# Bonus products and the group norm's transposes, issued after whole projections, in a one-core hybrid decoder layer

## The chip, the cores and the metric

The kernel runs on one core of one Trainium2 chip. The metric is the device time of one execution in microseconds (us). Its engines are named as the profile names them: PE (TensorE, matmuls and transposes), PEld (its weight loads), DVE (VectorE), ACT (ScalarE), POOL (GpSimd), and SP, which here only issues DMAs.

## The reference

One decoder layer over 512 tokens of width 1024, all in float32:

```
h      = rms_norm(x) * (1 + scale) + shift            # scale, shift from c
proj   = h @ w_in                                     # r, k, v, three low-rank inputs, conv u1/u2, gates a/b
r,k,v  = token_shift(proj[...])
y_a    = group_norm(rwkv7_scan(r, decay, k, v, -kk, kk*a)) * gn_gain + gn_bias
bonus  = sum_per_head(r * k * r_k) * v
y_a    = (y_a + bonus) * g
y_b    = silu(layer_norm(causal_conv31(u1 * sigmoid(u2))))
x      = x + gate * (concat(y_a, y_b) * sigmoid(gates)) @ w_out
x      = x + gate * relu(rms_norm(x)... @ w_ff_in)^2 @ w_ff_out
out    = rms_norm(x)
```

The change is about two lines of this: the bonus (a sum over each head of 64 channels, times v) and the group norm's output.

## The kernel before

The activations lie with channels on the 128 partitions and the 512 tokens along the free dimension. A **projection** (`proj`, L458) makes 128 output channels: two weight loads from HBM of 256 KB each into `raw_*`, a split of each into a high and a low part (`hi_*` on ACT, `lo_*` on POOL or DVE, L150 and L151), and then `mm3` (L163): 24 matmuls of 128x512 into one PSUM tile `ps_*` (lines 174, 175, 176 in turn, 8 times).

The 16 heads are worked on as 8 **pairs** j of two heads (128 channels), and two pairs make a **quarter** q of four heads. `rkv_pair(j)` makes the decay input `pzz` (L493), then the projections k, v, r of the pair, each followed by the token shift (`shift`, L464: ACT L465, then DVE L466). `prep_pair(j)` then forms, through small matmuls `pl` (L509), `pa` (L517) and `pn` (L524) and a chain of ACT and DVE instructions (L513 to L537), the scan's operands `AR` and `BK`, and last the **bonus**: L537 multiplies r, r_k and k into the tile `tr`; L539 is the matmul `pb`, which sums over each head with the block matrix `blk1` (`blk` in the trace); L541 multiplies by v into `bo`; L542 sends `bo` to the DRAM tile `bod[j]`. `tr` and `bo` have one buffer each (`bo` shares its tag `w1` with a tile that the next pair writes at L522).

For a quarter, `products` (L547) multiplies `AR` and `BK` into PSUM tiles `pA` (two banks, four chunks each, twice per pair) and masks them on DVE into `M` (L567); `solve` (L580) inverts small triangular blocks on DVE (62 instructions at L598 and L600); `merge_inverses`, `scan_operands` and `scan` follow, and `group_norm` (L707): statistics on DVE, 16 ACT instructions at L719 that normalise the tile `yq`, and then for each of the two pairs four transposes `pyt` (L724), a load of `bod[j]` (L726), one DVE instruction (L727) and a store to the DRAM tile `yad[j]` (L729), which `gate_a(j)` loads later.

The PSUM tag `m` of pool `pq` has two buffers. Of the loop's tiles, `pzz`, `pl`, `pa`, `pn`, `pb` and `pA` take them; `pyt` shares the one buffer of tag `y` with the scan's output `py`.

The order of the steps is a hand-written list, `ORDER` (L35): R is `rkv_pair`, I `products`, V `solve`, O `scan_operands`, M `merge_inverses`, S `scan`, Y `group_norm`, U two convolution projections (`u2`, then `u1`), T the 30 convolution taps on DVE (`cz`, L745), G `gate_a` with one projection `ga`, N, B, L, A, W later steps. It begins

```
U1:0v R0 R1:0v I0 U4 R2:0v R3 V0 T1:500 U3 M0 O0 T4 S0:2000 U2:0v I1:100 V1 O1:200 M1 T3:2000 Y0 R4
R5 G0 T2 U6:100 I2 V2:200 G1 S1:500 T6 U7 Y1 R6 M2 O2 R7 T7 I3:1000 V3:1000 U5 S2:100 O3 Y2 U0:100
```

The program is traced in this order; a number after a colon moves a step's instructions ahead by so many places. A planner then writes, before the program runs, one fixed list of instructions for each engine and for SP's DMA queue: it takes the earliest-traced instruction whose inputs it holds to be ready, by costs of its own. On the chip each engine runs its list in that order and waits where an input is late.

The functions that the change touches, and what calls them:

Of the kernel before, what the change touches and what calls it, by code (L numbers as in the profile page):

```python
# [8 lines left out]
F32 = mybir.dt.float32  # L9
# [3 lines left out]
ALU = mybir.AluOpType  # L13
# [5 lines left out]
P = 128  # L19
T = 512  # L20
# [42 lines left out]
def tile_rwkv7_conformer(  # L63
# [5 lines left out]
    nc = tc.nc  # L69
    V, S, G, PE = nc.vector, nc.scalar, nc.gpsimd, nc.tensor  # L70
# [14 lines left out]
    blk1 = const.tile([P, P], F32, name="blk1")  # L85
# [36 lines left out]
    hh = hp.tile([P, KT, T], F32R, name="hh")  # L122
    hl = hp.tile([P, KT, T], F32R, name="hl")
# [6 lines left out]
    def rsqrt_small(dst, v, tmp):  # L130

        V.tensor_scalar(dst.bitcast(I32), v.bitcast(I32), -0.5, 1597463007.0, op0=ALU.mult, op1=ALU.add)
        for _ in range(3):
            V.tensor_tensor(tmp, dst, dst, op=ALU.mult)
            V.scalar_tensor_tensor(tmp, tmp, -0.5, v, op0=ALU.mult, op1=ALU.mult)
            V.scalar_tensor_tensor(dst, tmp, 1.5, dst, op0=ALU.add, op1=ALU.mult)
# [17 lines left out]
    def wcol(src, c0, nm, eng=None, own=None):  # L154
        v = src.rearrange("(g k p) n -> g p k n", p=P, k=HK)
        out_ = []
        for g in range(2):
            raw = wp.tile([P, HK, P], F32, tag="wraw", name=f"raw_{nm}{g}")
            nc.sync.dma_start(out=raw, in_=v[g, :, :, c0:c0 + P])
            out_.append(split(raw, [P, HK, P], f"{nm}{g}", eng, own))  # L160
        return out_

    def mm3(ps, w, m):  # L163

        for k in range(KT):
            last = mm3k(ps, w, m, k)
        return last

    def mm3k(ps, w, m, k, ts_=slice(0, T), first=None):
        mh, ml = m  # L170
        wh, wl = w[k // HK]
        i = k % HK
        first = k == 0 if first is None else first
        PE.matmul(ps[:, ts_], wh[:, i, :], mh[:, k, ts_], start=first, stop=False, skip_group_check=True)  # L174
        PE.matmul(ps[:, ts_], wh[:, i, :], ml[:, k, ts_], start=False, stop=False, skip_group_check=True)  # L175
        return PE.matmul(ps[:, ts_], wl[:, i, :], mh[:, k, ts_], start=False, stop=(k == KT - 1),  # L176
                         skip_group_check=True)
# [9 lines left out]
    bod = [dram.tile([P, T], F32, name=f"bod{j}") for j in range(KT)]  # L187
# [55 lines left out]
    pq = cq.enter_context(tc.tile_pool(name="pq", bufs=1, space=PSUM, reuse_waits="tile"))  # L243
# [3 lines left out]
    with tc.tile_pool(name="e1", bufs=1) as e1, tc.tile_pool(name="e2", bufs=2) as e2:  # L247
# [11 lines left out]
        def load_ada(j):  # L259
            for s, o in ((1, D), (0, 0)):  # L260
# [19 lines left out]
                        op=ALU.add, axis=AX.X)  # L280
# [35 lines left out]
        for n, _, tag in EARLY:  # L316
            early[n] = (pq if tag == "y" else pp).tile([P, T], F32, tag=tag, name=f"ps_{n}",
                                                       bufs=2 if tag == "pp" else 1)
# [107 lines left out]
        for op in EORD.split():  # L426
            op, hp = (op + ":0").split(":")[:2]
# [25 lines left out]
    with ExitStack() as c1:  # L453
        lp = c1.enter_context(tc.tile_pool(name="lp", bufs=1, reuse_waits="tile"))
        qp = cq.enter_context(tc.tile_pool(name="qp", bufs=1, reuse_waits="tile"))
        tp = tpool[0] = cq.enter_context(tc.tile_pool(name="tp", bufs=1, reuse_waits="tile"))

        def proj(c0, nm):  # L458
            w = wcol(w_in2, c0, nm, lo_eng[0])
            ps = pp.tile([P, T], F32, tag="pp", name=f"ps_{nm}", bufs=2)  # L460
            mm3(ps, w, (hh, hl))
            return ps

        def shift(dst, ps, m):  # L464
# [15 lines left out]
        def chunks(t_):  # L480
            return t_.rearrange("p (c s) -> p c s", s=C)
# [22 lines left out]
        def prep_pair(j, rt, kt, vv, sg, WA):  # L504
            jc = slice(j, j + 1)

            pl = pq.tile([P, T], F32, tag="m", name=f"pl{j}", bufs=2)
            for tt in range(NT):
                PE.matmul(pl[:, tt * P:(tt + 1) * P], sg[:, tt, :], tri, start=True, stop=True)  # L509
            Pt = tp.tile([P, NCHK, 65], F32, tag="Pt", name=f"Pt{j}")  # L510
            Pi = tp.tile([P, NCHK, C], F32, tag="Pi", name=f"Pi{j}")
            G.memset(Pt[:, :, 0:1], 1.0)  # L512
            S.activation(Pt[:, :, 1:65], chunks(pl), AF.Exp, scale=-0.5 * ECON)  # L513
            S.activation(Pi, chunks(pl), AF.Exp, scale=0.5 * ECON)

            pa = pq.tile([P, T], F32, tag="m", name=f"pa{j}", bufs=2)
            PE.matmul(pa, WA[64:128, :], lo2[64:128, :], start=True, stop=True)  # L517
            at = tp.tile([P, T], F32, tag="sg", name=f"at{j}")
            S.activation(at, pa, AF.Tanh, bias=a0h[:, jc], scale=0.5)

            w1 = tp.tile([P, T], F32, tag="w1", name=f"w1_{j}")
            S.activation(w1, kt, AF.Square, scale=VEC["k_k"][:, jc])  # L522
            pn = pq.tile([P, T], F32, tag="m", name=f"pn{j}", bufs=2)
            PE.matmul(pn, blk1, w1, start=True, stop=True)  # L524
            S.activation(w1, pn, AF.Ln)
            S.activation(w1, w1, AF.Exp, scale=-0.5)
            V.scalar_tensor_tensor(w1, w1, 1e12, kt, op0=ALU.min, op1=ALU.mult)
            AR = qp.tile([P, NCHK, P], F32, tag="AR", name=f"AR{j}", bufs=4)
            BK = qp.tile([P, NCHK, P], F32, tag="BK", name=f"BK{j}", bufs=BKB)
            V.scalar_tensor_tensor(AR[:, :, 0:C], chunks(w1), kkn[:, jc], Pt[:, :, 0:C], op0=ALU.mult, op1=ALU.mult)  # L530
            V.scalar_tensor_tensor(w1, at, 1.0, w1, op0=ALU.add, op1=ALU.mult)
            V.scalar_tensor_tensor(BK[:, :, 0:C], chunks(w1), kkh[:, jc], Pi, op0=ALU.mult, op1=ALU.mult)
            S.activation(at, at, AF.Identity, scale=kah[:, jc], bias=ka1[:, jc])
            V.tensor_tensor(kt, kt, at, op=ALU.mult)
            V.tensor_tensor(BK[:, :, C:P], chunks(kt), Pi, op=ALU.mult)
            V.tensor_tensor(AR[:, :, C:P], chunks(rt), Pt[:, :, 1:65], op=ALU.mult)
            V.scalar_tensor_tensor(rt, rt, VEC["r_k"][:, jc], kt, op0=ALU.mult, op1=ALU.mult)  # L537
            pb = pq.tile([P, T], F32, tag="m", name=f"pb{j}", bufs=2)
            PE.matmul(pb, blk1, rt, start=True, stop=True)  # L539
            bo = tp.tile([P, T], F32, tag="w1", name=f"bo{j}")  # L540
            V.tensor_tensor(bo, pb, vv, op=ALU.mult)  # L541
            nc.sync.dma_start(out=bod[j], in_=bo)  # L542
            pc = qp.tile([P, NCHK, 1], F32, tag="pc", name=f"pc{j}", bufs=4)
            G.tensor_copy(pc, Pt[:, :, 64:65])
            return dict(AR=AR, BK=BK, v=vv, pc=pc, j=j)
# [161 lines left out]
        def group_norm(q, prs, yq, st):  # L707
            mv = qp.tile([P, NT * 4, 2], F32, tag="mv", name=f"mv{q}")
            rsd = qp.tile([P, NT * 4, 1], F32, tag="rsd", name=f"rsd{q}")
            for tt in range(NT):  # L710
                for h in range(4):
                    V.bn_aggr(mv[:, 4 * tt + h, :], st[:, tt, h:h + 1, :])
            rst = qp.tile([P, NT * 4, 1], F32, tag="rst", name=f"rst{q}")
            V.tensor_scalar(mv[:, :, 1:2], mv[:, :, 1:2], 64e-5, None, op0=ALU.add)
            rsqrt_small(rsd, mv[:, :, 1:2], rst)
            yv = yq.rearrange("p a h n -> p (a h) n")
            V.scalar_tensor_tensor(rst, mv[:, :, 0:1], -1.0, rsd, op0=ALU.mult, op1=ALU.mult)
            for i in range(NT * 4):
                S.activation(yv[:, i, :], yv[:, i, :], AF.Identity, scale=rsd[:, i, :], bias=rst[:, i, :])  # L719
            for pr, d in enumerate(prs):  # L720
                j = d["j"]
                pt = pq.tile([P, NT, P], F32, tag="y", name=f"pyt{q}{pr}")
                for tt in range(NT):
                    PE.transpose(pt[:, tt, :], yq[:, tt, 2 * pr:2 * pr + 2, :].rearrange("p h n -> p (h n)"), ident)  # L724
                yg = tp.tile([P, T], F32, tag="gy", name=f"yg{j}")
                nc.sync.dma_start(out=yg, in_=bod[j])  # L726
                V.scalar_tensor_tensor(yg, pt.rearrange("p a b -> p (a b)"), VEC["gn_gain"][:, j:j + 1], yg,  # L727
                                       op0=ALU.mult, op1=ALU.add)
                nc.sync.dma_start(out=yad[j], in_=yg)  # L729
# [259 lines left out]
        for op in ORDER.split():  # L989
            op, hp = (op + ":0").split(":")[:2]  # L990
# [5 lines left out]
    with tc.tile_pool(name="s3", bufs=2, reuse_waits="tile") as s3:  # L996
# [45 lines left out]
        for fq in range(NFQ):  # L1042
            fh = s3.tile([P, KT, T], F32R, tag="fh", name=f"fh{fq}")
            fl = s3.tile([P, KT, T], F32R, tag="fl", name=f"fl{fq}")
            for i in range(KT):
                if fq == 0 and i < NFF:
                    ps = first_ff[i]
                else:
                    w = wcol(w_ff_in[0], fq * D + i * P, f"fi{fq}{i}", G if fq == 0 and GFI > i else None)
                    ps = pp.tile([P, T], F32, tag="pp", name=f"ps_fi{fq}{i}", bufs=2)  # L1050
                    mm_last = mm3(ps, w, (hh, hl))
                f = s3.tile([P, T], F32, tag="f", name=f"f{fq}{i}")
# [8 lines left out]
            last = fq == NFQ - 1  # L1061
# [48 lines left out]
```

## Time and profile before

| what | value |
|---|---|
| median of 3 runs | 1126.58 us (1123.9 to 1131.93) |
| the profiled execution: its own time, and its span from the first to the last instruction | 1131.94 us, 1130.2 us |
| mean granted TensorE clock | 0.953 of full |
| PE busy, and PEld | 1023.5 us (91%), 792.5 us (70%) |
| DVE busy | 790.1 us (70%) |
| ACT, POOL busy | 479.1 us (42%), 198.2 us (18%) |
| DMA, mean over the span | 116 GB/s |

A row of the timeline has a start (us from the span's start), a duration (us), the engine, the line, the operation, the tile written and the tiles read, shapes and a count; in square brackets stands how long the engine was idle before it and what ended that. Neighbouring instructions of one line are merged into one row. A row of waits has the waiting instruction, what it waited for, the time in total, how many times and the longest. The four parts of the span are the load and first norm (up to about 75 us), the mixing layer's projections and scans (to about 600), the output projection with loads of the adaLN weights (to about 775), and the MLP.

### The profile page before, as it was taken

The page shows a single profiled execution, that of the slowest core. Times are in us where ns is not written, and L with a number is a line of the kernel's source. Part 1 is how long each engine was busy: PE and PEld are TensorE (multiplying, and loading weights), DVE is VectorE, ACT ScalarE, POOL GpSimd, SP SyncE. Part 2 cuts the span into 40 slices and gives each one's busy share as a digit, 9 for nine tenths or more (in the row PEclk, how much of TensorE's full clock was granted, in tenths as well). Part 3 has the DMA queues.
Part 4 walks back from the last instruction along what each step waited for, and adds up shares of the span by engine and source line. Part 5 has one row for each costly group of instructions (what it writes and reads, how often), then busy time and mean ns, then how long its engine had stood idle before and what let it go on. Part 6 is the DMA issues. An engine that isn't in the chain of part 4 may idle for free.

```text
span 1130.2 us, 16757 instructions
## 1 busy us (share of the span) xinstructions
PE 1023.5 (91%) x6037; PEld 792.5 (70%) x6037; DVE 790.1 (70%) x1622; ACT 479.1 (42%) x912; POOL 198.2 (18%) x191
## 2 busy tenths in 40 slices
PE   2999889889899789996997999899999999999995
PEld 1777666656677666665665767688888888888874
DVE  3859999969958997989455787585445445445557
ACT  5546445374644356534343433264323323423432
POOL 1123042222422533221121121200000000000002
PEclk9999999989999989996798999999999999999998
DMA  9622332331343234324257686731223323333332
GB/s 313 181 72 87 88 100 73 54 92 48 104 117 94 86 95 83 85 66 110 94 162 234 224 273 217 232 104 38 84 93 95 101 94 94 95 93 100 96 103 74
DMA packets 184605, 131.34 MB, mean 116 GB/s; under 512 B 49945, under 2 KB 152779, under 8 KB 184523
## 3 DMA queue, kind: packets, MB, share of 16 engines
q1 hardware_dynamic: 184523, 130.28, 39.1%
q8 instruction: 47, 0.77, 0.3%
q14 instruction: 35, 0.29, 0.1%
HBM read 116.61 MB, written 13.63 MB: 115 GB/s over the span
## 4 chain that ended last, share of the span: by engine, by line
PE 43%; DVE 16%; DMA 5%; issue 3%; ACT 3%; POOL 1%; SPq 0%; DVEq 0%; ACTq 0%; POOLq 0%
PE ps_fi L174 5%; PE ps_fi L175 5%; PE ps_fi L176 5%; DVE cz L745 5%; PE acc_fo L1005 4%; PE acc_fo L1004 4%; PE acc_fo L1003 4%; DMA ar<-in_ada_w_dram 2%; DVE tmp L598 1%; DVE aacc L217 1%; PE ps_ga L175 1%; PE ps_ga L176 1%; PE ps_ga L174 1%; DVE X L600 1%; PE pr L669 1%
## 5 line engine op out<-in xcount | busy, mean ns | idle before, releaser
L745 DVE SCALAR_TENSOR_TENSOR cz<-gl,cw,cz 128x512 f32<-128x512 f32 x240 | 200.8, 837 | 3.9 <-ACT cz L743 1.2
L151 DVE TENSOR_TENSOR lo_fo<-raw_fo,hi_fo 128x512 fp32r<-128x512 f32 x64 | 44.2, 691 | 92.1 <-ACT hi_fo L150 91.9
L175 PE MATMUL ps_fi<-hl,hi_fi 128*128 128x512 f32 (+1 forms) x288 | 105.6, 367 | 0.0
L176 PE MATMUL ps_fi<-hh,lo_fi 128*128 128x512 f32 (+1 forms) x288 | 105.3, 367 | 0.0
L174 PE MATMUL ps_fi<-hh,hi_fi 128*128 128x512 f32 (+1 forms) x288 | 105.0, 367 | 0.0
L1003 PE MATMUL acc_fo<-hi_fo,fh 128*128 128x512 f32 x256 | 101.3, 396 | 0.8 <-DVE t_fo L1010 0.8
L1004 PE MATMUL acc_fo<-lo_fo,fh 128*128 128x512 f32 x256 | 101.2, 395 | 0.0
L1005 PE MATMUL acc_fo<-hi_fo,fl 128*128 128x512 f32 x256 | 101.2, 395 | 0.0
L150 ACT CAST hi_fo<-raw_fo 128x512 fp32r<-128x512 f32 x64 | 39.7, 621 | 110.6 <-PE acc_fo L1005 87.8
L151 DVE TENSOR_TENSOR lo_fi<-raw_fi,hi_fi 128x512 fp32r<-128x512 f32 x64 | 43.8, 690 | 52.1 <-ACT hi_fi L150 51.2
L150 ACT CAST hi_fi<-raw_fi 128x512 fp32r<-128x512 f32 x64 | 39.9, 623 | 74.0 <-PE ps_fi L175 45.6
L1021 POOL TENSOR_TENSOR x<-x,fgain 128x512 f32<-128x512 f32 x4 | 5.5, 1392 | 363.8 <-ACT sq L1015 363.8
L175 PEld LDWEIGHTS ps_fi<-hl,hi_fi 128*128 128x128 f32 x288 | 54.3, 189 | 8.9 <-DVE hl L928 0.4
L176 PEld LDWEIGHTS ps_fi<-hh,lo_fi 128*128 128x128 f32 x288 | 54.3, 189 | 8.7
L174 PEld LDWEIGHTS ps_fi<-hh,hi_fi 128*128 128x128 f32 x288 | 54.0, 189 | 8.8 <-ACT hh L927 0.2
L174 PE MATMUL ps_u<-hh,hi_u 128*128 128x512 f32 x128 | 54.1, 422 | 5.4 <-DVE tr L466 2.9
L937 PE MATMUL acc_wo<-lo_wo,mh 128*128 128x512 f32 x128 | 53.0, 414 | 5.9 <-DVE lo_wo L151 3.2
L217 DVE SCALAR_TENSOR_TENSOR aacc<-ar,cact,aacc 128x512 f32<-128x512 f32 x56 | 49.9, 891 | 11.3 <-DMA ar<-in_ada_w_dram 10.7
L1003 PEld LDWEIGHTS acc_fo<-hi_fo,fh 128*128 128x128 f32 x256 | 48.2, 188 | 12.7 <-DVE t_fo L1010 1.3
L1005 PEld LDWEIGHTS acc_fo<-hi_fo,fl 128*128 128x128 f32 x256 | 48.2, 188 | 11.5
L1004 PEld LDWEIGHTS acc_fo<-lo_fo,fh 128*128 128x128 f32 x256 | 48.2, 188 | 11.5
L176 PE MATMUL ps_u<-hh,lo_u 128*128 128x512 f32 x128 | 54.9, 429 | 0.6 <-POOL Pt L512 0.6
(334 smaller groups left out, 2554.3 us busy)
## 6 DMA issues: line engine op xcount, KB each, us to landing
ar<-in_ada_w_dram SPq DMA_DIRECT2D x64, 256.0 KB
raw_fi<-in_w_ff_in_dram SPq DMA_DIRECT2D x64, 256.0 KB
raw_fo<-in_w_ff_out_dram SPq DMA_DIRECT2D x64, 256.0 KB
araw<-in_ada_w_dram SPq DMA_DIRECT2D x8, 1024.0 KB
raw_u<-in_w_in_dram SPq DMA_DIRECT2D x32, 256.0 KB
raw_wo<-in_w_out_dram SPq DMA_DIRECT2D x32, 256.0 KB
raw_k<-in_w_in_dram SPq DMA_DIRECT2D x16, 256.0 KB
raw_v<-in_w_in_dram SPq DMA_DIRECT2D x16, 256.0 KB
```

The lines of the kernel that those rows point to most:

```text
L150: S.copy(hi, raw)
L151: (eng or V).tensor_tensor(lo, raw, hi.bitcast(F32), op=ALU.subtract)
L174: PE.matmul(ps[:, ts_], wh[:, i, :], mh[:, k, ts_], start=first, stop=False, skip_group_check=True)
L175: PE.matmul(ps[:, ts_], wh[:, i, :], ml[:, k, ts_], start=False, stop=False, skip_group_check=True)
L176: return PE.matmul(ps[:, ts_], wl[:, i, :], mh[:, k, ts_], start=False, stop=(k == KT - 1), skip_group_check=True)
L217: eng.scalar_tensor_tensor(acc, a, cact[:, k:k + 1], acc, op0=ALU.mult, op1=ALU.add)
L598: V.tensor_tensor(tv, X[:, 0:n, s:s + 1].to_broadcast([P, n, m]), U[:, s:s + 1, s + 1:32].to_broadcast([P, n, m]), op=ALU.mult)
L745: V.scalar_tensor_tensor(cz, gl[:, w:w + T], cw[:, w * KT + j:w * KT + j + 1], cz, op0=ALU.mult, op1=ALU.add)
L937: PE.matmul(wacc[h][tt], mh[k][:, ts_], wl, start=False, stop=False)
L1003: PE.matmul(acc[tt], fh[:, k, ts_], wh, start=(n == 0), stop=False)
L1004: PE.matmul(acc[tt], fh[:, k, ts_], wl, start=False, stop=False)
L1005: PE.matmul(acc[tt], fl[:, k, ts_], wh, start=False, stop=(n == KT - 1))
```

## The change

`proj` counts. A list `pending` holds pairs of a counter and a function. Each call of `proj`, once it has traced its 24 matmuls, takes one off every counter, and traces the functions whose counter has come to zero, inside `tc.issue_after(last.ins)`: this makes every PE instruction that the function traces come after the projection's last matmul in PE's list (an edge of order alone, no wait for its end). Instructions of other engines in the function get no such edge; they take the place in the trace at which the function is called.

The bonus of a pair (the `pb` tile, L539, L541 and the store L542) becomes such a function with counter 1; L537, which fills `tr`, stays where it was. The second half of `group_norm` (transposes, L726, L727, L729) becomes `group_out` with counter 2 for quarters 0 to 2; for quarter 3 it is called at once, as before.

```diff
+        pending = []
+
         def proj(c0, nm):
             w = wcol(w_in2, c0, nm, lo_eng[0])
             ps = pp.tile([P, T], F32, tag="pp", name=f"ps_{nm}", bufs=2)
-            mm3(ps, w, (hh, hl))
+            last = mm3(ps, w, (hh, hl))
+
+            for e in list(pending):
+                e[0] -= 1
+                if e[0] == 0:
+                    pending.remove(e)
+                    with tc.issue_after(last.ins):
+                        e[1]()
             return ps
...
             V.scalar_tensor_tensor(rt, rt, VEC["r_k"][:, jc], kt, op0=ALU.mult, op1=ALU.mult)
-            pb = pq.tile([P, T], F32, tag="m", name=f"pb{j}", bufs=2)
-            PE.matmul(pb, blk1, rt, start=True, stop=True)
-            bo = tp.tile([P, T], F32, tag="w1", name=f"bo{j}")
-            V.tensor_tensor(bo, pb, vv, op=ALU.mult)
-            nc.sync.dma_start(out=bod[j], in_=bo)
+
+            def bonus():
+                pb = pq.tile([P, T], F32, tag="m", name=f"pb{j}", bufs=2)
+                PE.matmul(pb, blk1, rt, start=True, stop=True)
+                bo = tp.tile([P, T], F32, tag="w1", name=f"bo{j}")
+                V.tensor_tensor(bo, pb, vv, op=ALU.mult)
+                nc.sync.dma_start(out=bod[j], in_=bo)
+
+            pending.append([1, bonus])
...
+            if q < 3:
+                pending.append([2, lambda: group_out(q, prs, yq)])
+            else:
+                group_out(q, prs, yq)
+
+        def group_out(q, prs, yq):
             for pr, d in enumerate(prs):
```

In the order of the trace the bonus of pair 0 now comes after projection k1, of pair 1 after u2 of U4, of pair 2 after k3, of pair 3 after u2 of U3, of pair 4 after k5, of pair 5 after ga0, of pair 6 after k7, and of pair 7 after u2 of U5; the group norm's output of quarter 0 comes after v4, of quarter 1 after v6, of quarter 2 after u1 of U0. Between the old place and the new one lie `pzz` of pairs 1, 3, 5 and 7, `products` of quarter 0 (pairs 0 and 1) and `products` of quarter 3 (pairs 6 and 7).

## Rows read from the trace of the kernel before

**Rows 1.** The page's busy times, and the shares of the last-ending chain by engine.
```profile
PE 1023.5 (91%) x6037; PEld 792.5 (70%) x6037; DVE 790.1 (70%) x1622; ACT 479.1 (42%) x912; POOL 198.2 (18%) x191
...
PE 43%; DVE 16%; DMA 5%; issue 3%; ACT 3%; POOL 1%; SPq 0%; DVEq 0%; ACTq 0%; POOLq 0%
```

**Rows 2.** Windows: stretch, length, busy us by engine, granted clock, DMA share, GB/s.
```profile
75.00:225.00 150.00, 136.07 (x767) 102.95 (x766) 142.92 (x239) 73.51 (x131) 41.26 (x42) 0.94 0.31 81
...
350.00:525.00 175.00, 152.46 (x1124) 113.00 (x1123) 159.39 (x363) 81.37 (x166) 57.56 (x47) 0.94 0.33 84
```

**Rows 3.** Waits of PE: the bonus matmul, and the group norm's transposes.
```profile
PE pb L539 <- DVE tr L537: 13.9, 6, 5.0
...
PE pyt L724 <- ACT yq L719: 12.0, 6, 5.3
```

**Rows 4.** Timeline of PE around pair 2's bonus (k3 ends first).
```profile
155.14 0.39 PE L176 MATMUL ps_k<-hh,lo_k 128*128 128x512 f32 x1
...
165.49 2.08 PE L539 MATMUL pb<-tr,blk 128*128 128x512 f32 x2 [4.97 <-DVE tr L537]
...
167.35 1.91 PE L493 MATMUL pzz<-WD,tl 65*128 65x128 f32 x8
```

**Rows 5.** The same for pair 3, and for pair 6 with pair 7's decay input.
```profile
190.92 1.13 PE L539 MATMUL pb<-tr,blk 128*128 128x512 f32 x2 [2.31 <-DVE tr L537]
...
418.00 2.07 PE L539 MATMUL pb<-tr,blk 128*128 128x512 f32 x2 [4.02 <-DVE tr L537]
419.87 1.91 PE L493 MATMUL pzz<-WD,tl 65*128 65x128 f32 x8
```

**Rows 6.** Timeline of PE: the group norm's transposes of quarters 0 and 2.
```profile
286.77 0.33 PE L724 MATMUL pyt<-ident,yq 128*128 128x128 f32 x1 [1.38 <-ACT yq L719]
...
472.74 0.40 PE L176 MATMUL ps_u<-hh,lo_u 128*128 128x512 f32 x1
...
523.04 0.48 PE L724 MATMUL pyt<-ident,yq 128*128 128x128 f32 x1 [5.34 <-ACT yq L719]
```

**Rows 7.** Timeline of PE around pair 4's bonus, amid k5.
```profile
279.49 1.13 PE L539 MATMUL pb<-tr,blk 128*128 128x512 f32 x2 [1.73 <-DVE tr L537]
...
281.26 0.48 PE L176 MATMUL ps_k<-hh,lo_k 128*128 128x512 f32 x1
...
282.74 0.39 PE L176 MATMUL ps_k<-hh,lo_k 128*128 128x512 f32 x1
```

**Rows 8.** Timeline of PE around pair 5's bonus, amid ga0.
```profile
313.82 1.02 PE L539 MATMUL pb<-tr,blk 128*128 128x512 f32 x2
...
320.13 0.39 PE L176 MATMUL ps_ga<-hh,lo_ga 128*128 128x512 f32 x1
```

**Rows 9.** Timeline, quarter 0's products: pair 0's operand (DVE), pair 1's bonus, first product.
```profile
93.12 0.68 DVE L535 TENSOR_TENSOR BK<-tk,Pi 128x512 f32<-128x512 f32 x1
...
123.03 1.02 PE L539 MATMUL pb<-tr,blk 128*128 128x512 f32 x2
123.98 0.48 PE L184 MATMUL pA<-AR,BK 64*128 64x128 f32 x2
```

**Rows 10.** Timeline, quarter 3's products: pair 6 ready (DVE), pair 7's bonus, first product, last masks.
```profile
417.21 0.74 DVE L537 SCALAR_TENSOR_TENSOR tr<-tr,vt,tk 128x512 f32<-128x512 f32 x1
...
439.58 1.12 PE L539 MATMUL pb<-tr,blk 128*128 128x512 f32 x2 [0.68 <-DVE tr L537]
440.64 0.48 PE L184 MATMUL pA<-AR,BK 64*128 64x128 f32 x2
...
453.38 1.27 DVE L567 TENSOR_TENSOR M<-pA,mask 128x512 f32<-128x512 f32 x2
```

**Rows 11.** Waits of DVE from 75 to 530 us, on the two products.
```profile
DVE bo L541 <- PE pb L539: 5.3, 5, 2.8
DVE M L567 <- PE pA L184: 3.9, 3, 1.7
```

**Rows 12.** Waits of SP's DMA queue: the bonus's store.
```profile
SPq L542 <- DVE bo L541: 10.8, 3, 9.3
```

## The prediction

> **What bounds the kernel now.** I read the page first: PE is busy for 91% of the span, DVE for 70%, and the chain that ended last is 43% PE and 16% DVE [rows 1]. Those are averages over stages, and the change lies in one stage, the projections and scans between 75 and 600 us, so I read the windows next. There the picture turns: from 75 to 225 us DVE is busy for 142.92 of 150 us (95%) and PE for 136.07 (91%); from 350 to 525 us DVE has 159.39 of 175 (91%) and PE 152.46 (87%) [rows 2]. Two engines are nearly full together, each waiting now and then for the other; what PE gains in such a stretch it can lose again at its next wait for DVE. Third, the waits of PE: the bonus matmul `pb` waited 13.9 us in 6 waits for L537 on DVE, the transposes `pyt` 12.0 us in 6 for the ACT instructions of L719 [rows 3]. These two are PE's largest waits in the stage, and they are what the change names. The decisive view is the fourth, the timeline of PE around each of them: which projection's matmuls stand ahead of the waiting instruction already.
>
> **Part 1: the edges.** Each edge demands a place behind the last matmul of one named projection. For pair 2 that is k3. Its last matmul starts at 155.14; `pb` follows at 165.49, ten microseconds later, with most of v3 ahead of it as well [rows 4]. The place that the change asks for is the place it has. I went through all eleven. The bonuses of pairs 0, 1, 2, 3, 6 and 7 stand behind their projection already, and so do the transposes of quarters 0, 1 and 2: for quarter 2 the projection ends at 472.74 and the transposes start at 523.04 [rows 6]. So nine of eleven edges move nothing, and the long waits stay where they are: 4.97 us at pair 2, 2.31 at pair 3, 4.02 at pair 6, 5.34 at quarter 2, 1.38 at quarter 0 [rows 4 to 6]. The planner put these instructions late; DVE or ACT was later still, and an edge to an earlier projection doesn't change that. Cost and gain: 0.
>
> Two edges do move something. **Pair 4**: `pb` stands amid k5 after a wait of 1.73 us, with seven matmuls of k5 behind it (281.26 to 282.74, 0.25 us each, some 1.7 us) [rows 7]. They will go first and fill the wait. But PE's next wait, 1.38 us for ACT at 286.77 [rows 6], ends when ACT ends, and PE would only come to it earlier. Bounds: 0 to -1.73; I take 0, since that wait for ACT is what is late next. **Pair 5**: `pb` runs at 313.82 without a wait; ga0 ends at 320.13, so it moves by 6.3 us [rows 8]. Its DVE instruction and its store move with it. On DVE nothing that is queued then depends on `bo`, and the longest wait that DVE has for a `pb` is 2.8 us [rows 11], which could vanish. SP's queue is the danger: it issues in order, and waited up to 9.3 us for a `bo` before it could issue the weight loads behind that store [rows 12]. If the store's place in SP's list moved less than the data, the loads behind would be late by up to the 6.3 us. The planner moves both by the same matmuls, so I take 0, with -2.8 and +6.3 as bounds.
>
> **Part 2: the two buffers of tag m.** This is the change's real content. Tiles of that tag come in the order of the trace, not as they are ready. Pair 6's last operand is formed before the L537 at 417.21, so its products `pA` could have run from 418; they start at 440.64, right behind `pb` of pair 7 at 439.58 [rows 10]. Pair 0's operand is there at 93.8, its products start at 123.98, right behind `pb` of pair 1 at 123.03 [rows 9]. And `pzz` of the next pair follows `pb` directly at 167.35 and at 419.87 [rows 4, 5] (four times in all, pairs 1, 3, 5 and 7). Tracing `pb` later takes it out of the way of these:
>
> - `pzz` of pairs 3 and 7 (1.91 us each [rows 4, 5]) can run ahead of `pb`, in time that PE otherwise waits. At pair 7 it stands at the head of that pair's chain: -1.9. At pair 3 DVE is 95% busy, so I count half, -0.95, with 0 and -1.9 as bounds. Pairs 1 and 5 have little or no wait there: 0.
> - Quarter 3's products: those of pair 6 move up by about ten microseconds, into pair 7's chain of ACT and DVE work, and only pair 7's remain behind it. DVE waited 3.9 us for products, in 3 waits [rows 11], and `pb` itself, 1.06 us (439.58 to 440.64 [rows 10]), leaves the path: between 0 and -5.0. The masks end at 454.65 [rows 10], and what follows is convolution taps that DVE would do in any case; I take half of the 3.9, -2.0.
> - Quarter 0's products: the same with 0.95 us (123.03 to 123.98 [rows 9]), in the fullest stretch of DVE: half, -0.5; bounds 0 and -0.95.
>
> What comes later for it: `pb` of pairs 1 and 7 now waits for the masks of both pairs' products, some 10 us, and so does the store of `bo`. For pair 7 nobody needs either soon. For pair 1, `tr` and `w1` must be free for pair 2, whose r projection starts long after; 0.
>
> **Sum**: -1.9 - 0.95 - 2.0 - 0.5 = -5.35 us, about -5.4. Against the profiled execution's own 1131.94 us that is 1126.5. That execution is 5.4 us over the median of 1126.58, near the slowest of the three, so I apply the difference to the median: **1121.2 us**, rounded 1121. With all bounds at one end: -1.73 - 2.8 - 3.8 - 5.0 - 0.95 = -14.3, 1112; at the other +6.3, 1133.
>
> **Rivals.**
>
> *The change does what it says* and both waits go: 13.9 + 12.0 us at the most [rows 3], 1126.58 - 25.9 = **1101**. For it: these are PE's largest waits in the stage. Against: nine of eleven edges are met already. It would need the planner, with its lists shifted, to place `pb` and `pyt` several microseconds later than now. Chance 0.12.
>
> *DVE bounds the stage and nothing changes*: **1127**. Everything that PE wins is waited away at the next DVE result, since DVE's own work is the same, instruction for instruction. For it: 95% and 91% [rows 2]. Against: DVE's 3.9 + 5.3 us of waits for `pA` and `pb` [rows 11] are time that DVE itself loses. The Trainium skill (Perfetto Trace Analysis, Identifying the Most-Contended Engine) says to improve the engine with the highest occupancy, and to judge TensorE by its weight loads and not by matmul time. By that rule TensorE has room (102.95 of 150 us, 69%, against DVE's 95% [rows 2]) and a new order on its list alone would bring 0; the trace agrees on which engine is fuller. Chance 0.2.
>
> *The waits move from `pb` to `pA`, and the kernel is slower.* The products of quarters 0 and 3 now stand earlier, amid projections, and the second half of each pair's products needs the masks that DVE makes of the first half. If the planner believes DVE quicker than it is, as it did at every `pb`, PE stops in front of them with the projections queued behind. There are four such places (two pairs in each quarter). At the mean wait of a `pb`, 13.9 / 6 = 2.3 us, this costs 9.3; at the longest, 5.0, it costs 20 [rows 3]. The middle, 14.6, less the 5.4 of the forecast is +9: **1136**, from 1130 to 1141. It decides once the masks come more than about 1.3 us late on average (5.4 / 4). For it: DVE is fullest just there. Against: the products waited for DVE so little before that PE's list of long waits doesn't hold them. Chance 0.18.
>
> **How the numbers follow.** Forecast 0.5, rivals 0.12, 0.2 and 0.18. A measurement of this kernel tells about 1% (11.3 us: under 1115.3 or over 1137.8) from no change. Faster by more: the first rival's 0.12 and the low end of the forecast's own range (1112 to 1133), about 0.06: 0.18. Slower by more: the upper half of the third rival, 0.09, and 0.03 for a store that holds up SP's queue together with it: 0.12. Within: 0.7. The range leaves out most of the first rival and the far end of the third, under 0.2 together: 1105 to 1138.
>
> **What would show it.** Right: `pzz` of pairs 3 and 7 ahead of `pb` of pairs 2 and 6; `pA` of pair 6 before 435 and of pair 0 before 120; waits of PE for L537 still above 8 us, and for L719 still above 8 us. First rival: those two waits under 3 us each. Second: the same moves, and the span within 2 us. Third: waits of `pA` for L567 of 8 us or more, where PE had hardly any. Wrong altogether: if `pA` still follows `pb` of pairs 1 and 7, tag m isn't what held it; or if the span changes by much with these waits alike, the cause lies in a part of the lists that I take as unmoved, most likely SP's queue.

## The result and the profile after

The changed kernel is slower: 1135.64 us at the median of 10 runs, against 1130.51 us for 10 runs of the kernel before on the same chip. The ratio of the mean times is 1.006, with an interval from 1.0033 to 1.0088, which is 4 to 10 us. Forecast was 1121.2 us, 5.4 us less. The time lies in the predicted range and within the 1% that was called "same", but it moved the other way. The profiled execution of the changed kernel took 1139.53 us, with a span of 1137.5 us.

The page of the changed kernel, busy times and the chain by engine, answers to [rows 1]:

```profile
PE 1019.2 (90%) x6037; PEld 787.4 (69%) x6037; DVE 790.2 (69%) x1622; ACT 479.7 (42%) x912; POOL 198.2 (17%) x191
...
PE 35%; DVE 7%; DMA 6%; ACT 2%; issue 2%; POOL 0%; SPq 0%; DVEq 0%; ACTq 0%; POOLq 0%
```

No engine has more work than before; VectorE's 790.2 us are 790.1 in the kernel before. So time was lost by waiting. The two windows of [rows 2], in the changed kernel, and the stretch between them, first before the change and then in the changed kernel, say where:

```profile
75.00:225.00 150.00, 135.64 (x799) 102.39 (x798) 143.65 (x241) 76.52 (x138) 41.17 (x42) 0.98 0.32 82
...
225.00:350.00 125.00, 113.77 (x1034) 82.56 (x1032) 97.18 (x238) 70.63 (x145) 35.40 (x35) 0.96 0.35 92
...
225.00:350.00 125.00, 115.49 (x1064) 83.92 (x1062) 102.73 (x251) 72.26 (x147) 38.66 (x37) 0.99 0.37 96
...
350.00:525.00 175.00, 145.67 (x1063) 107.69 (x1062) 150.36 (x345) 76.61 (x153) 55.52 (x45) 0.94 0.31 80
```

The first is nearly as it was (143.65 us of VectorE's work, before 142.92). Between 225 and 350 us the changed kernel does 5.6 us more of it than the kernel before. From 350 to 525 us it does 150.36 us where there were 159.39, so VectorE idles 9 us longer there: it loses the lead, and at 525 us it is 2.8 us of work behind. TensorE's waits in the changed kernel, which answer to [rows 3], don't show that:

```profile
PE pyt L743 <- ACT yq L732: 15.1, 8, 5.0
PE pb L550 <- DVE tr L546: 14.5, 4, 5.9
...
PE pA L184 <- DVE M L580: 1.3, 5, 0.4
```

The two waits that the change names are still there, and the products hardly wait. The timeline of TensorE in the changed kernel shows that the order did change as foretold [rows 5, 9, 10]:

```profile
106.57 0.49 PE L184 MATMUL pA<-AR,BK 64*128 64x128 f32 x2
...
396.29 0.61 PE L502 MATMUL pzz<-WD,tl 65*128 65x128 f32 x4
...
409.64 2.07 PE L550 MATMUL pb<-tr,blk 128*128 128x512 f32 x2 [5.93 <-DVE tr L546]
...
422.06 0.49 PE L184 MATMUL pA<-AR,BK 64*128 64x128 f32 x2
...
438.98 1.13 PE L550 MATMUL pb<-tr,blk 128*128 128x512 f32 x2
```

`pzz` of pair 7 goes ahead of pair 6's `pb` (396.29, before 419.87). Quarter 3's products start at 422.06 (before 440.64), and pair 7's `pb` comes behind them. Now to the engine that lost time. VectorE's timeline in the kernel before, 440 to 450 us:

```profile
440.75 0.69 DVE L541 TENSOR_TENSOR bo<-pb,tv 128x512 f32<-128x512 f32 x1 [0.67 <-PE pb L539]
442.57 1.29 DVE L567 TENSOR_TENSOR M<-pA,mask 128x512 f32<-128x512 f32 x2 [1.13 <-PE pA L184]
443.77 0.68 DVE L738 SCALAR_TENSOR_TENSOR gl<-gl,ps_u 128x512 f32<-128x512 f32 x1
445.45 1.29 DVE L567 TENSOR_TENSOR M<-pA,mask 128x512 f32<-128x512 f32 x2 [1.00 <-PE pA L184]
```

And in the changed kernel, 438 to 456 us, the times in brackets being idle time and what ended it:

```profile
438.23 1.29 DVE L580 TENSOR_TENSOR M<-pA,mask 128x512 f32<-128x512 f32 x2 [1.36 <-PE pA L184]
440.14 0.69 DVE L552 TENSOR_TENSOR bo<-pb,tv 128x512 f32<-128x512 f32 x1 [0.62 <-PE pb L550]
447.18 0.69 DVE L757 SCALAR_TENSOR_TENSOR gl<-gl,ps_u 128x512 f32<-128x512 f32 x1 [6.35 <-PE ps_u L176]
452.25 0.43 DVE L713 COPY RV<-pn 64x256 f32<-64x256 f32 x1 [4.38 <-PE pn L704]
...
455.00 1.54 DVE L764 SCALAR_TENSOR_TENSOR cz<-gl,cw,cz 128x512 f32<-128x512 f32 x2 [1.87 <-ACT cz L762]
```

`gl` is the input of a tile's convolution taps, 30 of them on VectorE; it needs that tile's two projections `u2` and `u1` from TensorE. The tap ahead of the 30 is an instruction of ScalarE, which has it in its own list; for tile 5, before and in the changed kernel:

```profile
449.31 0.80 ACT L743 ACTIVATE cz<-gl,vt,cw 128x512 f32<-128x512 f32 x1
...
454.15 0.81 ACT L762 ACTIVATE cz<-gl,vt,cw 128x512 f32<-128x512 f32 x1
```

In the kernel before, tile 5's last `ps_u` runs between the first products: `gl` waits for nothing at 443.77, no gap around the masks is over 2 us, and from 450 on there are taps at hand, nine in the next 10 us. In the changed kernel the masks are over before 440, tile 5's projections end at 447, behind the last of the products, and VectorE stands for 6.35 us; then it waits 4.38 us for a matmul of the scan and 1.87 for ScalarE, and has done three taps by 460. The taps alone, in windows, are counted in VectorE's column. Before:

```profile
425.00:475.00 50.00, 0.66 (x4) 0.42 (x4) 25.71 (x26) 0.80 (x1) 1.00 0.39 87
475.00:525.00 50.00, 0.66 (x4) 0.42 (x4) 23.17 (x30) 0.81 (x1) 0.91 0.30 73
525.00:545.00 20.00, 1.12 (x4) 0.72 (x4) 8.47 (x12) 0.00 (x0) 0.50 0.38 119
```

The same windows in the changed kernel:

```profile
425.00:475.00 50.00, 0.66 (x4) 0.42 (x4) 10.93 (x12) 0.81 (x1) 1.00 0.35 79
475.00:525.00 50.00, 1.05 (x4) 0.83 (x4) 29.54 (x35) 0.81 (x1) 0.92 0.29 74
525.00:545.00 20.00, 1.11 (x4) 0.71 (x4) 10.48 (x14) 0.00 (x0) 0.50 0.44 125
```

Taps fall from 26 to 12 in the first 50 us and are made up later, among the scan's own steps. The changed kernel is 6 to 8 us ahead at most steps between 385 and 433 us. Quarter 3's solve starts 12.4 us earlier (456.5, before 468.8), yet its last multiplication starts where it did (506.9, before 507.1). At quarter 2's transposes the lead is gone (524.36, [rows 6] 523.04), at the next scan stage (`px`) the kernel is 4.2 us behind, at the first matmul of the output projection 4.0, at the first FFN matmul 8.2. So in this pair of traces half of the distance comes only after 616 us; in e1 below, whose lists are the same, 7.1 us are there at the output projection already.

### The profile page after: what moved, and what is told of

Same layout as the page of the kernel before. It is cut to its first block, busy times and chain, and to the rows that moved or that the text cites. A ratio compares the mean times of both kernels' runs of the same rounds, so it can differ in the third digit from the quotient of the medians.

```text
span 1137.5 us, 16744 instructions
## 1 busy us (share of the span) xinstructions
PE 1019.2 (90%) x6037; PEld 787.4 (69%) x6037; DVE 790.2 (69%) x1622; ACT 479.7 (42%) x912; POOL 198.2 (17%) x191
## 4 chain that ended last, share of the span: by engine, by line
PE 35%; DVE 7%; DMA 6%; ACT 2%; issue 2%; POOL 0%; SPq 0%; DVEq 0%; ACTq 0%; POOLq 0%
PE ps_fi L174 5%; PE ps_fi L175 5%; PE ps_fi L176 5%; PE acc_fo L1024 4%; PE acc_fo L1023 4%; PE acc_fo L1022 4%; DMA ar<-in_ada_w_dram 2%; PE acc_wo L957 1%; PE acc_wo L956 1%; DMA mr<-mgd 1%; DVE aacc L217 1%; PE acc_wo L955 1%; DMA z<-czd 1%; PE ps_ga L174 1%; DMA raw_fi<-in_w_ff_in_dram 1%
## 5 line engine op out<-in xcount | busy, mean ns | idle before, releaser
L764 DVE SCALAR_TENSOR_TENSOR cz<-gl,cw,cz 128x512 f32<-128x512 f32 x240 | 203.0, 846 | 5.1 <-ACT cz L762 2.7
L217 DVE SCALAR_TENSOR_TENSOR aacc<-ar,cact,aacc 128x512 f32<-128x512 f32 x56 | 45.5, 813 | 13.9 <-DMA ar<-in_ada_w_dram 13.4
```

The source lines that it names most:

```text
L217: eng.scalar_tensor_tensor(acc, a, cact[:, k:k + 1], acc, op0=ALU.mult, op1=ALU.add)
L764: V.scalar_tensor_tensor(cz, gl[:, w:w + T], cw[:, w * KT + j:w * KT + j + 1], cz, op0=ALU.mult, op1=ALU.add)
```

## The experiments

The theory after reading the traces was that pair 7's bonus alone does the harm: traced behind quarter 3's products, it pulls them ahead of tile 5's projections. The rivals were that the time is lost only behind 600 us, and that the edges cost. Each kernel was timed against the kernel before on the same chip: e1 to e4 on one, e5 to e8 on a second, e9 to e11 on a third. This table gathers what the runs gave; taps and VectorE's busy time are those of 425 to 475 us, and "first tap" is when ScalarE starts tile 5's first tap. The kernel before was profiled in an execution of 1131.94 us, 4 to 6 us over its medians in the three later batches, and the profiled executions of e4, e5, e7 and e11 (1132.61, 1130.99, 1127.20, 1128.69 us) are no slower than it or hardly so: a few us between two traces decide nothing, only the ratios do.

| kernel | pair 7's bonus | taps | DVE busy us | first tap, us | ratio to before |
|---|---|---|---|---|---|
| before | at once | 26 | 44.25 | 449.3 | 1 |
| changed | deferred | 12 | 34.47 | 454.2 | 1.006 [1.0033, 1.0088] |
| e1 no edges | deferred | 14 | 34.95 | 457.3 | 1.0074 [1.0046, 1.0102] |
| e2 all but pair 7 | at once | 25 | 41.66 | 446.6 | 0.9982 [0.9957, 1.0007] |
| e3 pair 7 alone | deferred | 15 | 35.49 | 458.1 | 1.0126 [1.0092, 1.0159] |
| e4 tile 5 ahead | deferred | 22 | 37.79 | 442.7 | 1.0041 [1.0016, 1.0066] |
| e5 quarter 3 unhurried | deferred | 16 | 35.16 | 454.1 | 1.0063 [1.0041, 1.0085] |
| e6 even pairs | at once | 21 | 42.34 | 444.5 | 0.9983 [0.9962, 1.0003] |
| e7 pair 1 alone | at once | 26 | 43.85 | 450.5 | 1.0027 [1.0007, 1.0047] |
| e8 norm alone | at once | 28 | 44.26 | 445.8 | 1.0025 [1.0005, 1.0045] |
| e11 two projections | at once | 23 | 40.11 | 450.2 | 1.0042 [1.0018, 1.0066] |

**e1: the deferral without its edges.**

```diff
-                    with tc.issue_after(last.ins):
-                        e[1]()
+                    e[1]()
```

> The deferral stays, but without the edge of order: the functions are only traced later. The planner's lists for every engine come out the same as the changed kernel's, instruction for instruction. Theory 1 (pair 7's bonus, traced behind quarter 3's products, pushes U5's projections back on PE, and DVE runs out of work from 441 to 455 us): ratio to before 1.003 to 1.009, as the changed kernel; DVE's wait for gl after 440 us about 6 us again. Theory 2 (the loss comes after 600 us, from DMA and POOL in the stage of the output projection, whatever the lists before): the same ratio, but the distance to before at 530 us near 0 and 5 or more at 750. Theory 3 (the edges themselves cost): 1.000.

In the traces TensorE, VectorE, ScalarE and GpSimd run the changed kernel's instructions in the same order, and the time is the same within the intervals: 1.0074. The edges do nothing, not even for pairs 4 and 5, whose later place comes from the tracing alone; that rival falls. The idle time is the same in this execution too (VectorE's timeline):

```profile
450.37 0.69 DVE L756 SCALAR_TENSOR_TENSOR gl<-gl,ps_u 128x512 f32<-128x512 f32 x1 [6.32 <-PE ps_u L176]
455.44 0.43 DVE L712 COPY RV<-pn 64x256 f32<-64x256 f32 x1 [4.39 <-PE pn L703]
```

**e2: everything deferred but pair 7's bonus.**

```diff
-            pending.append([1, bonus])
+            if j == 7:
+                bonus()
+            else:
+                pending.append([1, bonus])
```

> The changed kernel with pair 7's bonus traced in its old place; all else is deferred. u1 of U5 ends at place 1838 of PE's list, as before the change (1912 in the changed kernel). Theory 1: DVE's wait for gl near 440 us is gone (under 1 us), the lead of 7 us that the changed kernel had at 420 us is kept in part, ratio 0.993 to 1.000. Theory 2: as the changed kernel, 1.003 to 1.009. Theory 3: about 1.004.

The loss is gone, 0.9982. Products start at 435.9 us, `gl` of tile 5 comes at 439.1 without a wait, and 25 taps are done by 475 us:

```profile
425.00:475.00 50.00, 0.66 (x4) 0.42 (x4) 23.65 (x25) 0.82 (x1) 1.00 0.37 88
475.00:525.00 50.00, 1.11 (x4) 0.71 (x4) 24.95 (x33) 0.82 (x1) 0.86 0.29 77
```

**e3: pair 7's bonus alone deferred, the norm as before.**

```diff
-            pending.append([1, bonus])
+            if j in (7,):
+                pending.append([1, bonus])
+            else:
+                bonus()
...
-            if q < 3:
+            if False:
```

> Only pair 7's bonus is deferred, all else as before the change. u1 of U5 ends at place 1898 of PE's list. Theory 1: no lead at 420 us, and the wait of DVE for gl near 445 us comes (3 us or more): ratio 1.003 to 1.010. Theory 2: 1.000 to 1.004, with any loss after 600 us. Theory 3: 1.000 to 1.002.

The single bonus costs 1.26%, twice the whole change. Quarter 3's products come 12.9 us early, the solve 9.2, and VectorE again finds nothing to do. But `gl` of tile 5 has waited only 1.70 us for its projection, not the 3 or more that theory 1 expected. VectorE stands for 10.02 us between `gl` and the tile's taps, because the first tap on ScalarE is late:

```profile
448.20 0.69 DVE L760 SCALAR_TENSOR_TENSOR gl<-gl,ps_u 128x512 f32<-128x512 f32 x1 [1.70 <-PE ps_u L176]
...
458.06 0.82 ACT L765 ACTIVATE cz<-gl,vt,cw 128x512 f32<-128x512 f32 x1
...
458.91 0.75 DVE L767 SCALAR_TENSOR_TENSOR cz<-gl,cw,cz 128x512 f32<-128x512 f32 x1 [10.02 <-ACT cz L765]
```

ScalarE has `gl` from 448.9 us on, and until 458.06 it makes copies, above all of the scan's operands (`BT`, `RV`) and for quarter 3's products (`M`, `AR`), partly waiting for TensorE's transposes; its list has the tap behind them. In the kernel before, the tap comes 4.9 us behind `gl`. So in e3 most of the delay reaches VectorE through ScalarE's list. No run moved that one instruction, so how much of the loss it carries isn't shown.

The rival that the loss comes behind 600 us falls for e3: the last tap's transposes are 17.5 us late at 552 us already.

**e4: the changed kernel with tile 5's projections ahead.**

```diff
-I3:1000 V3:1000 U5 S2:100
+I3:1000 V3:1000 U5:1000 S2:100
```

> The changed kernel with the step U5 moved ahead by 1000 places (U5:1000), so that its projections go before quarter 3's products (first 24 matmuls end at place 1751, the second 24 at 1780 of PE's list). Theory 1: gl of U5 is there before 420 us, DVE never waits for it, the convolution taps fill DVE from 430 to 455 us: ratio 0.990 to 1.000. Theory 2: 1.003 to 1.009. If moving the products themselves is what helps and U5's lead takes their place: about 1.000.

A miss: 1.0041, not below 1. `gl` of tile 5 comes at 430.7 and 22 taps are done by 475 us, but now quarter 3's products end at 457.9 (changed kernel 437.9), the solve starts at 474.7 and the next `px` is 8.3 us late (a lateness that is down to 1.1 us at quarter 3's transposes, 590 us, in this trace). VectorE's waits in 425 to 545 us:

```profile
DVE gl L757 <- PE ps_u L176: 4.3, 2, 4.0
DVE cst L771 <- PE pz L769: 3.1, 1, 3.1
```

The wait of 4.0 us is for tile 5's own projection, at 430.73. Then `gl` lies unused for 11 us: ScalarE, held by pair 7's r projection until 432.25, works off that pair's chain and scan operands, and comes to tile 5's first tap only then:

```profile
442.67 0.80 ACT L762 ACTIVATE cz<-gl,vt,cw 128x512 f32<-128x512 f32 x1
```

So lateness of tile 5's projections by itself isn't the cause, and having `gl` early isn't yet having taps. I read it so: products and projections feed VectorE through one TensorE, and whichever goes first as a block leaves VectorE short of the other. That is argued, not shown.

**e5: quarter 3's products and solve without their priority,** to part that from the rival that the early solve takes VectorE from the taps.

```diff
-I3:1000 V3:1000 U5 S2:100
+I3 V3 U5 S2:100
```

> The changed kernel with the priority of 1000 taken from quarter 3's products and solve in the order by hand (I3:1000 V3:1000 becomes I3 V3). TensorE's list keeps quarter 3's first product at place 1748, as in the changed kernel, but spreads the rest to 1916; U5's projection of u1 ends at place 1930, later still than in the changed kernel (1912; before 1838); VectorE's list has the first step of quarter 3's solve at place 790, as in the kernel before (791; changed 776). Theory A (U5's projections come late on TensorE, so VectorE has no taps between 440 and 455 us): a wait of VectorE for ps_u of 5 us or more stays and the ratio to before is 1.006 or more. Theory B (the solve comes early and takes VectorE from the taps, which then come late and are not hidden): the solve's first step falls back to about 465 to 470 us and the ratio is 0.997 to 1.001.

1.0063, as A said, but A's sign is missing: the wait is not for `ps_u`. It moved to the products, which now lie between projections:

```profile
DVE M L580 <- PE pA L184: 10.1, 3, 4.1
DVE RV L713 <- PE pn L704: 2.0, 1, 2.0
```

`gl` comes at 452.1, later than in the changed kernel (447.2), as its place in the list said. The solve starts at 463.7 us, 7 us later than in the changed kernel though short of the 465 that B named, and it is no faster: B in its form of an early solve falls. What stays is the late first tap and VectorE's idle time, whatever it waits for.

**e6, e7, e8: what the other parts do.** Bonuses of pairs 0, 2, 4 and 6 alone, pair 1's alone, and the norm alone (e6 and e7 leave the norm as before, by the second edit of e3; the cut shows the line that differs):

```diff
-            pending.append([1, bonus])
+            if j in (0, 2, 4, 6):     # e6; e7: (1,); e8: (), norm deferred
+                pending.append([1, bonus])
+            else:
+                bonus()
```

> The kernel before with the bonuses of pairs 0, 2, 4 and 6 alone deferred by one projection; pairs 1, 3, 5, 7 and the group norm as before. pzz of pairs 1, 3, 5, 7 go ahead of pb of pairs 0, 2, 4, 6, and quarters 0 and 3's products keep their places (387 and 1791 of TensorE's list; before 388 and 1798), but U5's u1 ends at place 1890 (before 1838, changed 1912). Theory A (U5 late on TensorE starves VectorE): a wait for ps_u near 445 us of 3 us or more, and a ratio of 1.003 to 1.007. Theory B (quarter 3's products early): ratio 0.997 to 1.001. If the even pairs make the lead: pzz of pairs 3 and 7 earlier by 15 us or more, lead of 2 to 3 us at 400 us.

> The kernel before with pair 1's bonus alone deferred. TensorE's list has quarter 0's products at places 332 to 424 (before 388 to 445) and is the same from place 445 or so up to 1730 apart from that. Both theories: ratio 0.996 to 1.001. If the lead of 5 to 6 us that the changed kernel has at 290 us comes from quarter 0's products, it shows here at 290 and 400 us (4 to 6); if it comes from the pzz of the odd pairs, at most 1 us is here.

> The kernel before with the group norm's transposes alone deferred by two projections. The lists of TensorE, VectorE and the DMA queue are those of before but for a few places near the transposes of quarter 2 and SP's rows of the bonuses. All theories: ratio 0.999 to 1.001, every milestone within 1 us up to 520 us.

e6 has tile 5's `u1` at place 1890 of TensorE's list, and theory A said 1.003 to 1.007 for that; it measured 0.9983, with `gl` at 443.4, where the kernel before has it (443.8), and a wait of 0.2 us. So the place in TensorE's list doesn't say how late an instruction runs; of A's lateness in time e6 is no test. e7 measured 1.0027: quarter 0's products are 18.0 us earlier (106.0) and nothing comes of it; at 290 us the kernel is 2.6 us behind, not 4 to 6 ahead. e8 measured 1.0025. Up to 475 us its TensorE list is that of the kernel before, and still its profile runs 3.5 us ahead from 280 to 440 us. So leads of that size between two profiles mean nothing, and of the changed kernel's 6 to 8 us about half may be such. I found no place in e7's and e8's traces for a loss of 0.25%, which their intervals only just part from none; what it is stays open.

**e9 and e10: ten of tile 5's taps left out,** in the changed kernel and in the kernel before.

```diff
-            for w in range(1, CW):
+            for w in range(1, CW - 10 if j == 5 else CW):
```

> The changed kernel with ten of the convolution's taps of tile 5 left out (CW - 10 in place of CW for j == 5; these ten are missing from the output, and nothing else is changed). In the profile of the changed kernel ps 240 taps take 203.0 us, 846 ns each, so VectorE has 8.5 us less to do before the last tap. Theory B2 (in this stage the set of VectorE's work up to the last tap, with its idle time, sets the end, and the changed kernel loses because it idles VectorE 6 to 10 us near 440 to 475 us): the last tap comes 6 to 9 us earlier than in the changed kernel (536.1 us), and the ratio to before falls from 1.006 to 0.998 to 1.001. Rival C (TensorE, 90% busy, sets the end, and VectorE's idle time near 445 us is only a sign of it): the last tap moves but the time doesn't, ratio 1.003 to 1.008.

> The kernel before with the same ten taps of tile 5 left out. Theory B2: VectorE sets the end of this stage in the kernel before too, so the same 8.5 us come off: ratio 0.991 to 0.995. Rival C: ratio 0.998 to 1.002. A middle way, that VectorE's freed time is filled by other waits in the kernel before (it is 95% busy from 425 to 500 us) but not in the changed one: 0.996 to 0.998.

e9: 0.9997 [0.9978, 1.0017], so 0.63% or 7.1 us less than the changed kernel, give or take 4 by the two intervals. e10: 0.9963 [0.9941, 0.9986], 4.2 us less, 1.6 to 6.7. The ten taps were expected to be 8.5 us of work; in the traces the time in taps falls by 7.2 us (203.0 to 195.8) and 5.8 (200.8 to 195.0). VectorE's work before the last tap counts in both, where rival C expected nothing. The midpoints say nearly all of it in the changed kernel and half or more in the kernel before, the middle way; the intervals don't part the two. The idle time at `gl` is as it was in e9 (6.3 and 4.4 us): the taps that it delays are what was taken out. The last tap came at 531.1 us, 5.0 earlier than in the changed kernel, just short of the 6 to 9 expected.

**e11: bonuses of pairs 0 to 6 behind two projections, pair 7's at once.**

```diff
-            pending.append([1, bonus])
+            if j == 7:
+                bonus()
+            else:
+                pending.append([2, bonus])
```

> The changed kernel with the bonuses of pairs 0 to 6 behind two projections in place of one, and pair 7's at once. The first products of quarters 0 and 3 keep the places that they have in the kernel whose pair 7 alone isn't deferred (332 and 1788; there 332 and 1797), and U5's u1 ends at 1902 (there 1838). If the wait of TensorE for the bonus's operand (14.5 us in the changed kernel) is a loss that a longer deferral removes, that wait falls under 8 us and the ratio is 0.988 to 0.994. Theory B2 (VectorE sets the end of the stage; TensorE's waits for it only move): the wait may fall, but the ratio is 0.996 to 1.003, as with one projection (0.998).

TensorE's wait doesn't fall:

```profile
PE pb L550 <- DVE tr L546: 14.4, 5, 6.8
```

So a longer deferral doesn't bring what the first rival promised. But 1.0042 misses the other range too. `gl` of tile 5 comes at 449.5 us, 23 taps are done by 475, and VectorE waits 4.7 us in 425 to 545 us for matmuls of the scan (`RV` for `pn`). Pair 7's bonus is at once here, so its deferral isn't the only thing that costs. I take the mechanism to be of the same kind, which is not shown; its size I had not foreseen.

## Why the prediction was wrong

- *The edges cost and gain nothing.* Right: e1 has the same order and time. Pairs 4 and 5, which I thought the edges would move, aren't moved by them; the later tracing moves them.
- *The real content is the order of the two buffers of tag m.* Right. All moves came as written: `pzz` of pairs 3 and 7 ahead of `pb`, pair 6's products at 422.06 (before 435 was asked), pair 0's at 106.57 (before 120). The waits for L537 and L719 stayed, 14.5 and 15.1 us.
- *`pzz` and quarter 0's products, -1.9, -0.95 and -0.5.* Together -3.35 us, a ratio of 0.997. e2, which holds just these and the norm, gave 0.9982 [0.9957, 1.0007]: not refuted, and not told from nothing. For quarter 0 alone e7 measured no gain.
- *Quarter 3's products, -2.0.* This is the step that failed. "What follows is convolution taps that DVE would do in any case" took the taps as there whenever VectorE is free. They need `gl`, which needs two projections on TensorE that the earlier products push behind them (a wait of 6.35 us in the changed kernel, 1.70 in e3), and a first tap on ScalarE, which comes at 454.2 and 458.1 us (before 449.3). What the term counted did come: VectorE's waits for quarter 3's products fell from 3.9 to 1.4 us. "For pair 7 nobody needs either soon" was true of `pb` and asked the wrong question: pair 7's `pb` had held the products back, and with that had let tile 5's projections through. Between e1 and e2, which differ in pair 7's bonus (and in edges that do nothing), the term measures 1.0074 - 0.9982 = 0.92%, or +10.4 us in place of -2.0; my bounds of 0 to -5.0 excluded a loss without a reason from a row.
- *The rival of waits at `pA`* had the right sign and the wrong place: TensorE's wait there is 1.3 us, not 9 to 20. The price was paid on VectorE.
- *The rival that VectorE bounds the stage* fits e9 and e10 on the engine, and was wrong that then nothing changes. The Trainium skill (Perfetto Trace Analysis, Identifying the Most-Contended Engine) says to improve the engine with the highest occupancy first. The prediction drew from it that a new order on TensorE's list alone would bring 0. The trace agrees on which engine is fuller, but e3 shows 1.26% from one bonus traced later, with VectorE's work the same. The order of VectorE's and ScalarE's lists moved along with TensorE's: the less full engines decide when the fuller one is fed.
- *What would show it*: every sign listed for the forecast came true while the time went the other way. All of them were on TensorE. The last sign listed also came: the span changed by 7.3 us with these waits alike. It blamed SP's queue, and there the traces show no cause: SP's waits before the bonus's store, whatever ended them, fell from 19.2 to 13.7 us in total, and in 420 to 475 us none of TensorE's listed waits is for weights, in the kernel before or in the changed one. The one that was missing for the loss is VectorE's busy time from 425 to 475 us, 44.25 us before and 34.47 after.

Not settled is how the idle time becomes the final distance. From 425 to 475 us VectorE loses 9.8 us, part of which is the lead that it had, and the runs lose 6.8 (0.6%); e4 and e11 lose 0.4% with 6.5 and 4.1 us. The table orders pair 7's two cases, not every kernel within them. Tile 5's first tap orders the kernels better: the four latest, 454.1 to 458.1 us, are the four slowest. e4, with the earliest, doesn't fit.

## What to carry to other kernels

Where one engine is 90% busy and a second one feeds it from two streams, ask of every move on the second what work the first will have left in the next ten microseconds, and trace it back to its inputs through every engine's list (here TensorE's projections and one instruction on ScalarE); "work that is there anyway" has to be found in the timeline. An instruction that holds a buffer and so delays a ready stream may be what lets the other stream through: before taking it away, look which matmuls stand in its shadow. Such a part can be tried alone; e2 and e3 parted by 1.4% what one change had mixed.

## What the runs showed of the hardware

TensorE's granted clock fell to 0.50 of full speed, its lower level of 1.2 GHz, at the end of this stage, in all 13 traces, and how soon it rose again differs. In the kernel before, TensorE was busy for 2.71 of the 5 us at whose end the clock fell and 0.95 of the next 5, and full from 535 us on:

```profile
515.00:520.00 5.00, 2.71 (x12) 1.89 (x11) 5.00 (x11) 0.46 (x1) 1.29 (x1) 0.97 0.40 61
520.00:525.00 5.00, 0.95 (x2) 0.36 (x2) 4.89 (x10) 2.78 (x9) 0.00 (x0) 0.50 0.34 50
...
535.00:540.00 5.00, 5.00 (x20) 3.50 (x20) 3.92 (x17) 1.17 (x3) 1.27 (x1) 0.50 0.42 143
540.00:545.00 5.00, 5.00 (x30) 3.43 (x29) 1.36 (x8) 0.15 (x1) 0.00 (x0) 0.50 0.22 68
```

In e6, where the last tap comes 4 us earlier (529.7 us), it is full from 530 us on, and at full clock from 535 us:

```profile
530.00:535.00 5.00, 5.00 (x22) 3.93 (x22) 3.69 (x15) 0.96 (x2) 0.00 (x0) 0.59 0.34 105
535.00:540.00 5.00, 5.00 (x52) 3.62 (x50) 2.23 (x12) 1.20 (x3) 0.76 (x1) 1.00 0.31 107
```

In the same 5 us, 535 to 540, TensorE is full in both kernels, and gets through 52 matmuls at the upper level and 20 at the lower (of mixed shapes, so not a ratio of speeds). So VectorE's lateness at the last taps may be paid again on TensorE, in the pass that follows. No run changed the clock by itself, so that isn't shown, and the changed kernel doesn't bear it out: its clock is back at full in the same 5 us as before, 550 to 555.

The listed runs say how far the clock goes with the time. Over the 23 runs of the kernel before that e1 was compared with, the time is 7.3 us shorter for each 0.01 more of mean granted clock (correlation -0.90). e1's mean clock is 0.001 lower than theirs, so by this estimate some 7 of the 7.9 us between the means remain at the same clock. e10's is 0.005 higher, and only about 1 of its 4.2 us remains: in the kernel before, fewer taps and a higher clock can't be told apart.
